# A hybrid decoder layer on one core: fewer warming transposes, the first weights cast in halves, the last operand sum traced later

## The chip, the cores and the metric

The kernel runs on one core of one Trainium2 chip. The metric is the device time of one execution in microseconds, the median of several runs. Engines are named as in the profile: PE is TensorE, DVE is VectorE, ACT is ScalarE, POOL is GpSimd, SP is SyncE, which here issues most transfers.

## The reference

One step of a one-layer decoder over a prompt of 512 tokens and 8 sequences of 4 sampled tokens, with a matrix-memory branch (mLSTM) and a sliding-window attention side by side, gates, a merge and a layer norm. The part that this change touches is the input projection of prompt and samples (544 rows together):

```python
def _in_proj(x, w_in, b_igate, b_fgate):
    u = jnp.einsum('btd,dc->btc', x, w_in)
    ...
    q_m, k_m, v_m, o_m, z_m, q_a, k_a, v_a, z_a, g_m, g_a, i_pre, f_pre = parts
```

`w_in` has 2048 rows and 18952 columns, all in float32.

## The kernel before, in words

**Products.** TensorE is fed with fp32r operands, so each float32 operand is split in a high part, a cast, and a low part, the difference. `split` does this for a weight tile of 8 x 128 rows and 128 columns (`wh` by ACT in L208, `wl` by DVE in L209), and `hilo` for the tokens (L254 and L255). A product is then three matmuls: high by high, high by low, low by high. `wh` and `wl` have two buffers each, so a cast waits until the tile two before it has been used up.

**Tokens first.** The prompt comes in five column pieces (L316): 256, 256, 512, 512 and 512 of its 2048 columns; between them stand the loads of the first weight tiles (`raw`, 512 KB each). PE transposes 128 columns at a time (L337) into one of four PSUM buffers `sm`, and ACT and DVE split them: column blocks 0 to 7 go to `a11` (tokens 0 to 271) and `a21` (the others), blocks 8 to 15 to `xk`. Ahead of all this PE makes warming transposes of a constant (L304), whose result nobody reads.

**Two plain column groups.** The loop at the end of the shown part makes two groups of 128 columns (attention values) by `gemm`: 16 steps over the column blocks, with both halves of the tokens in two PSUM banks. The first group's first weight cast carries `behind`, a pin: the scheduler may not put it before a given cast of the tokens.

**Pairs.** All other columns of `w_in` are made in pairs by `paired`, with seven products in place of eight: the tokens and column blocks are cut in two, and sums of quarters are multiplied (`s1`, `n2`, `n3`, `s4` and the quarters themselves, list `XS`). Step n of a pair uses `XS[n]`; its 24 matmuls of 272 tokens go to one of three banks (`BANK`), several steps add into the same bank, and after each step `gather` evacuates (L704 to L723). Step 4 and step 6 share a bank: step 6 may add only after step 4's evacuation (L719) has read. The sums of tokens are made by the generator `x_sums`: `s1`, `n3`, `n2` while the plain groups run, and `s4` last (L609 to L611), after the mark `plain_done`.

**Order.** What is written in the code is only a preference: a scheduler places the instructions of each engine by priorities (`high_priority`), dependencies and pins (`issue_after`). Generators that were spawned advance one step at each `tick`, so where a generator stands decides the priority of what it issues. On each engine the resulting order is fixed; an instruction that waits holds all behind it.

## Time and profile before

| | |
|---|---|
| median of 3 runs | 2447.45 us (2445.05 to 2449.03) |
| profiled execution | 2445.12 us |
| its span, first to last instruction | 2443.2 us |
| PE busy in the span | 2428.3 us, 99% |
| DVE, ACT, POOL busy | 78%, 51%, 22% |
| TensorE clock granted | 0.999 of full |

The profile belongs to one execution, which is near the lower end of the runs. PE's share is so high that the interest lies in the few places where it waits. In the timeline a row gives the start, the busy time, the engine, the line, the operation, the tiles written and read, the count, and in brackets the idle time before it with what ended it. A busy share of PE does not say that it is at its peak; so the prediction looks at the distance from one matmul to the next.

### The profile page before, as it was taken

To read this page: it belongs to the slowest core of one execution; us is meant where nothing else is said; L and a number is where in the kernel's file an instruction comes from. 1 tells how busy PE (TensorE), PEld (TensorE's weight loads), DVE (VectorE), ACT (ScalarE), POOL (GpSimd) and SP (SyncE) were. 2 spreads that over 40 slices of the span, in tenths; PEclk is the share of its full clock that TensorE was granted. 3 is DMA by queue.
4 is the path that set the end of the run, shared out by engine and by line. 5 is a ranking of instruction groups with operands and counts; after the bars stand their busy time and mean duration, and the time that the engine had idled before them with its cause. 6 is when DMAs were issued, how large, how long until landed. Compare 5 with 4: busy or idle time off the path is not lost.

```text
span 2443.2 us, 49028 instructions
## 1 busy us (share of the span) xinstructions
PE 2428.3 (99%) x19394; PEld 2373.8 (97%) x19394; DVE 1913.3 (78%) x2880; ACT 1251.2 (51%) x2073; POOL 533.4 (22%) x504
## 2 busy tenths in 40 slices
PE   8999999999999999999999999999999999999999
PEld 8999999999999999999999999999999999999998
DVE  7768888888888888887877888878766576877666
ACT  6456676676566665533433444544644444434432
POOL 4114334333333431211111221120000120111111
PEclk9999999999999999999999999999999999999999
DMA  6876666667777655677687676687755598898776
GB/s 180 205 173 157 161 164 145 160 156 174 169 172 177 165 144 146 153 226 235 184 253 235 176 235 216 183 246 222 252 178 191 164 256 241 232 234 270 204 216 204
DMA packets 569501, 479.62 MB, mean 196 GB/s; under 512 B 48632, under 2 KB 464232, under 8 KB 569016
## 3 DMA queue, kind: packets, MB, share of 16 engines
q1 hardware_dynamic: 550520, 410.69, 57.1%
q0 software_dynamic: 17840, 64.23, 13.5%
q8 instruction: 152, 2.49, 0.4%
q10 hardware_dynamic: 912, 1.57, 0.2%
q14 instruction: 77, 0.63, 0.1%
HBM read 326.35 MB, written 100.77 MB: 175 GB/s over the span
## 4 chain that ended last, share of the span: by engine, by line
PE 97%; DMA 1%; DVE 1%; ACT 0%; issue 0%; SPq 0%; DVEq 0%; ACTq 0%
PE bank L694 49%; PE bank L696 24%; PE bank L218 10%; PE sm L1522 2%; PE sm L218 2%; PE bank L1329 1%; PE sm L1556 1%; PE sm L809 1%; PE sm L1572 1%; PE sm L860 1%; PE sm L2011 1%; PE sm L835 1%; PE sm L1334 1%; DMA xr<-in_x_prompt 0%; PE bank L418 0%; DMA kb<-in_state_attn_k 0%
## 5 line engine op out<-in xcount | busy, mean ns | idle before, releaser
L208 ACT CAST wh<-raw 128x1024 fp32r<-128x1024 f32 x641 | 671.8, 1048 | 829.5 <-PE bank L694 718.2
L209 DVE TENSOR_TENSOR wl<-raw,wh 128x1024 fp32r<-128x1024 f32 x641 | 802.0, 1252 | 202.7 <-ACT wh L208 186.6
L694 PE MATMUL bank<-xk,wh 128*128 128x272 f32 x2336 | 323.3, 289 | 0.0
L674 DVE TENSOR_TENSOR raw<-raw,raw 128x1024 f32<-128x1024 f32 x244 | 310.6, 1274 | 7.5 <-DMA raw<-in_w_in 1.9
L694 PEld LDWEIGHTS bank<-xk,wh 128*128 128x128 f32 x2336 | 303.4, 188 | 1.9 <-issue 1.4
L713 POOL TENSOR_TENSOR ev<-p,ev 128x272 f32<-128x272 f32 x85 | 116.8, 1375 | 458.0 <-ACT ev L712 432.8
L696 PE MATMUL bank<-xk,wl 128*128 128x272 f32 x1168 | 170.0, 287 | 0.0
L694 PE MATMUL bank<-n2h,wh 128*128 128x272 f32 x656 | 170.0, 291 | 0.0
L694 PE MATMUL bank<-n3h,wh 128*128 128x272 f32 x656 | 169.5, 291 | 0.2 <-ACT wh L208 0.2
L694 PE MATMUL bank<-s1h,wh 128*128 128x272 f32 x656 | 169.6, 291 | 0.0
L694 PE MATMUL bank<-n2l,wh 128*128 128x272 f32 x656 | 167.9, 287 | 0.0
L694 PE MATMUL bank<-n3l,wh 128*128 128x272 f32 x656 | 167.7, 288 | 0.0
L694 PE MATMUL bank<-s4h,wh 128*128 128x272 f32 x656 | 167.4, 289 | 0.0
L694 PE MATMUL bank<-s1l,wh 128*128 128x272 f32 x656 | 167.3, 287 | 0.0
L694 PE MATMUL bank<-s4l,wh 128*128 128x272 f32 x656 | 167.0, 287 | 0.0
L696 PEld LDWEIGHTS bank<-xk,wl 128*128 128x128 f32 x1168 | 155.6, 188 | 0.1
L672 POOL DMA_DIRECT2D raw<-raw x96 | 83.4, 868 | 314.6 <-DVE ev L721 210.2
L694 PE MATMUL bank<-a11h,wh 128*128 128x272 f32 x584 | 150.4, 289 | 0.0
L694 PE MATMUL bank<-a11l,wh 128*128 128x272 f32 x584 | 149.5, 288 | 0.0
L694 PEld LDWEIGHTS bank<-n3h,wh 128*128 128x128 f32 x656 | 123.4, 188 | 2.1 <-issue 1.2
L694 PEld LDWEIGHTS bank<-s1h,wh 128*128 128x128 f32 x656 | 123.2, 188 | 1.6 <-issue 1.0
L694 PEld LDWEIGHTS bank<-n2h,wh 128*128 128x128 f32 x656 | 123.3, 188 | 1.2 <-issue 1.2
(546 smaller groups left out, 5804.5 us busy)
## 6 DMA issues: line engine op xcount, KB each, us to landing
raw<-in_w_in SPq DMA_DIRECT2D x296, 512.0 KB
raw<-raw POOLq DMA_DIRECT2D x96, 512.0 KB, 5.0
C<-in_state_mlstm_C SPq DMA_DIRECT2D x32, 1024.0 KB
out<-C SPq DMA_DIRECT2D x64, 512.0 KB
raw<-in_w_proj_a SPq DMA_DIRECT2D x32, 512.0 KB
raw<-in_w_proj_m SPq DMA_DIRECT2D x32, 512.0 KB
raw<-in_w_out SPq DMA_DIRECT2D x32, 512.0 KB
d_v<-ev SPq DMA_DIRECT2D x16, 272.0 KB
```

The costliest lines, as they stand in the source:

```text
L208: state["cast"] = A.copy(wh[:, k:k + n], raw[:, k:k + n])
L209: state["split"] = V.tensor_tensor(out=wl[:, k:k + n], in0=raw[:, k:k + n], in1=r32(wh[:, k:k + n]), op=ALU.subtract)
L218: PE.matmul(ps[f][:, :w], a[:, kk], b(k, c, w), start=(k == 0 and n == 0), stop=(k == 15 and n == 2))
L672: G.dma_start(out=w[out][:], in_=w[b][:], accum_op=ALU.add)
L674: V.tensor_tensor(out=w[out][:], in0=w[a][:], in1=w[b][:], op=ALU.add)
L694: PE.matmul(ps, wh[:, k], x(p, k), start=(first and k == 0 and p == 0), stop=False, skip_group_check=True)
L696: state["end"] = PE.matmul(ps, wl[:, k], x(0, k), start=False, stop=(k == 7), skip_group_check=True)
L713: G.tensor_tensor(out=c22, in0=p1, in1=c11, op=ALU.subtract)
L809: PE.matmul(pp[:, c0 + w0:c0 + 256], qs[a][:, j * 128:j * 128 + 128], kx[:, k0:k0 + 256 - w0], start=(n == 0), stop=(n == 1))
L835: PE.transpose(pt[:, b * 128:b * 128 + 128], s_[:, b, 128:256], ident)
L860: PE.matmul(po[:, b * 128:b * 128 + n], VA[:, b], p_[:, 2 * b:2 * b + n // 128], start=(b == 0 and m == 0), stop=(b == 3 and m == 1), skip ...
L1522: state["cells"] = PE.matmul(pp[:, 0:258], a[:, b * 128:b * 128 + 128], b_[:, b, f], start=(b == 0 and n == 0), stop=(b == 3 and n == 2))
```

## The change

Ten warming transposes instead of twenty. The pin of the first weight cast is the cast of column block 2 instead of 3, and that tile is split in two halves of 4 x 128 rows (`parts` 2 for the first half tile of the first group). The last operand sum leaves `x_sums`, becomes a generator of its own, and is spawned with the pairs: its pieces are issued in the ticks of the first pair's steps, each pinned behind the last weight split, and `paired` runs out what is left of it ahead of step 4's product.

```diff
-    for _ in range(20):
+    for _ in range(10):
         PE.transpose(warm[:, 0:128], ident, ident)
...
-                if k == 3:
-                    state["k3"] = state["x_cast"]
+                if k == 2:
+                    state["k2"] = state["x_cast"]
...
-        while not state.get("plain_done"):
-            yield
-        s4 = S["s4"] = quad(act, "s4")
+    def last_sum():
+        s4 = S["s4"]
         for ch in range(4):
...
-            V.tensor_tensor(out=n2r[:, ks_], in0=h12, in1=n2r[:, ks_], op=ALU.subtract)
-            V.tensor_tensor(out=n2r[:, ks_], in0=n2r[:, ks_], in1=l12, op=ALU.add)
+            with tc.issue_after(state["split"].ins):
+                V.tensor_tensor(out=n2r[:, ks_], in0=h12, in1=n2r[:, ks_], op=ALU.subtract)
+                V.tensor_tensor(out=n2r[:, ks_], in0=n2r[:, ks_], in1=l12, op=ALU.add)
             hilo(n2r[:, ks_], s4[0][:, ks_], s4[1][:, ks_])
             yield
...
-                  before=gates_between if kk else None, ps=[sm(), sm()] if kk else None, behind=state["k3"])
+                  before=gates_between if kk else None, ps=[sm(), sm()] if kk else None, behind=state["k2"], parts=(1 if kk else 2, 1))
...
-    state["plain_done"] = True
     for _ in sums_:
         pass
+    S["s4"] = quad(act, "s4")
...
-    paired(work)
+    rest_ = last_sum()
+    spawn(rest_)
+    paired(work, rest=rest_)
```

What this does to the order of the instructions, at the three places that the prediction speaks of. In these rows a number behind a name tells one buffer or use from another; the changed kernel's lines from 603 on are one lower (L718 there is L719 in the profile).

PE at the very beginning, before. `sm_30` to `sm_32` are the transposes of the third column piece, `wh_44` and `wl_45` the first weight tile:

```order
L304 MATMUL sm_13_140<-cc_78 128x128 x20
L337 MATMUL sm_29_223<-cc_78,xr_16_168 128x128 x4
L340 MATMUL bank_25_188<-cc_78,xs_14_161 128x128 x4
L337 MATMUL sm_30_238<-cc_78,xr_18_172 128x128 x4
L218 MATMUL bank_42_369<-a11h_3_114,wh_44_371 128x272
L218 MATMUL bank_43_370<-a21h_5_116,wh_44_371 128x272
L218 MATMUL bank_42_369<-a11l_4_115,wh_44_371 128x272
L218 MATMUL bank_43_370<-a21l_6_117,wh_44_371 128x272
L337 MATMUL sm_31_248<-cc_78,xr_18_172 128x128 x4
```

The same place now (the rows of the first three blocks' transposes, and the repeats of the three products for blocks 1 to 3, are not shown):

```order
L304 MATMUL sm_13_140<-cc_78 128x128 x10
L337 MATMUL sm_29_213<-cc_78,xr_16_158 128x128 x4
L340 MATMUL bank_25_178<-cc_78,xs_14_151 128x128 x4
L218 MATMUL bank_42_359<-a11h_3_114,wh_44_361 128x272
L218 MATMUL bank_42_359<-a11l_4_115,wh_44_361 128x272
L218 MATMUL bank_42_359<-a11h_3_114,wl_45_362 128x272
L218 MATMUL bank_43_360<-a21h_5_116,wh_44_361 128x272
L337 MATMUL sm_30_228<-cc_78,xr_18_162 128x128 x4
```

Before, the third piece's first transposes stood ahead of every product. Now twelve products on `a11` and one on `a21` stand ahead of them. Later in the same queue, from the fifth piece's transposes on, the rows are in the old order.

DVE in the first pair, now, from the split of step 3's weights (`wl_95`) to that of step 6 (`wl_111`). L609 and L610 make the sum `n2r`, L255 with `s4l` its low half, L453 to L461 are small operations of the gates, L714 and L718 are evacuations:

```order
L209 TENSOR_TENSOR wl_95_793<-raw2_84_743,wh_94_792 128x1024
L255 TENSOR_TENSOR s4l_70_715<-n2r_137,s4h_69_714 128x544
L610 TENSOR_TENSOR n2r_137<-n2r_137,xk2_9_120 128x544
L714 SCALAR_TENSOR_TENSOR ev_98_823<-bank_101_836,p1_93_786 128x272
L209 TENSOR_TENSOR wl_100_833<-raw_82_739,wh_99_832 128x1024
L609 TENSOR_TENSOR n2r_137<-xk2_8_119,n2r_137 128x544
L209 TENSOR_TENSOR wl_103_888<-raw2_83_741,wh_102_887 128x1024
L610 TENSOR_TENSOR n2r_137<-n2r_137,xk2_10_121 128x544
L454 RECIPROCAL t_75_720<-t_75_720 128x17
L718 SCALAR_TENSOR_TENSOR ev_98_823<-bank_101_836,ev_98_823 128x272
L209 TENSOR_TENSOR wl_111_939<-raw2_84_743,wh_110_938 128x1024
```

Not shown are further rows of the same kinds: from the split ahead of these (`wl_91`) to L718 there are four splits, eight sums, two low halves and five small operations; the last sum stands between L454 and L718, and the other two low halves behind `wl_111`. Before, no row of the last sum stood here: all twelve were done ahead of the first pair's second split.

PE where the first pair's step 5 (`s4`, `wh_102`) and step 6 (`wh_110`) meet, now:

```order
L693 MATMUL bank_96_797<-s4l_70_715,wh_102_887 128x272
L693 MATMUL bank_96_797<-s4h_69_714,wh_102_887 128x272
L693 MATMUL bank_101_836<-xk2_7_118,wh_110_938 128x272
L693 MATMUL bank_101_836<-xk2_9_120,wh_110_938 128x272
L695 MATMUL bank_101_836<-xk2_8_119,wl_111_939 128x272 x4
L695 MATMUL bank_96_797<-s4h_69_714,wl_103_888 128x272 x8
L693 MATMUL bank_121_1046<-a11h_3_114,wh_114_971 128x272
```

Step 6 was behind all 24 matmuls of step 5. Now nine of step 5 come first, then the 24 of step 6, then the other fifteen of step 5, and behind them the second pair's first product (`wh_114`). On ACT the third and fourth piece's casts (`s4h`) stand behind the cast of `wh_110` and ahead of that of `wh_114`.

## The prediction

> **What bounds the kernel now.** I read the page's first part, the waits of TensorE (PE) over the whole span, and then PE's timeline at the beginning, where all three edits lie.

> ```profile
> PE 2428.3 (99%) x19394; PEld 2373.8 (97%) x19394; DVE 1913.3 (78%) x2880; ACT 1251.2 (51%) x2073; POOL 533.4 (22%) x504
> ```
> ```profile
> PE sm L304 <- DMA cc<-in_consts: 3.4, 1, 3.4
> PE bank L218 <- DVE c L1759: 2.9, 1, 2.9
> PE sm L337 <- DMA xr<-in_x_prompt: 2.3, 1, 2.3
> PE sm L1026 <- DMA kb<-in_state_attn_k: 1.0, 1, 1.0
> PE bank L218 <- DVE xk L255: 0.5, 1, 0.5
> ```

> PE sets the time: all its listed waits together are some 10 us of 2443, and those of the first 200 us are the three on `cc`, `xr` and `xk`. The first ends before any edit can act. So at most 2.3 + 0.5 = 2.8 us can be won here, 0.11%; whatever PE loses in the later steps is lost in full, since it has no other slack.

> ```profile
> 3.37 4.53 PE L304 MATMUL sm<-cc 128*128 128x128 f32 x20 [3.37 <-DMA cc<-in_consts]
> 7.69 2.02 PE L337 MATMUL sm<-cc,xr 128*128 128x128 f32 x16
> 9.54 0.60 PE L340 MATMUL bank<-cc,xs 128*128 128x128 f32 x4
> 12.49 0.63 PE L337 MATMUL sm<-cc,xr 128*128 128x128 f32 x4 [2.34 <-DMA xr<-in_x_prompt]
> ...
> 26.75 0.50 PE L218 MATMUL bank<-xk,wh 128*128 128x272 f32 x2
> 27.75 0.52 PE L218 MATMUL bank<-xk,wh 128*128 128x272 f32 x2 [0.50 <-DVE xk L255]
> ```

> The reader is to see two gates. At 12.49 the third block of prompt columns lands; from there PE is dense until 27.25. At 27.75 it has waited for the low half of column block 12 (`xk`), and from there on it is dense again.

> **Ten transposes fewer.** The twenty start between 3.37 and 7.69, 0.216 us apart. The ten that go are worth 2.2 us on PE, so the first column block's transposes start near 5.5 if their data are there (bounds 5.5 and 7.69; the trace shows only that they did not wait at 7.69). PE then waits longer for what lands at 12.35: alone this edit gives nothing, it lets ACT and DVE begin the column splits earlier.

> **The first weights in halves, behind the third column block.**

> ```profile
> 11.51 1.04 ACT L208 CAST wh<-raw 128x1024 fp32r<-128x1024 f32 x1
> ```
> ```profile
> 12.59 1.23 DVE L209 TENSOR_TENSOR wl<-raw,wh 128x1024 fp32r<-128x1024 f32 x1 [0.61 <-ACT wh L208]
> ```
> ```profile
> 120.00:200.00 80.00, 80.00 (x643) 79.97 (x644) 56.88 (x80) 47.05 (x80) 19.62 (x17) 1.00 0.70 171
> ```

> ACT had no idle time before its cast at 11.51, so the weights had landed by then. With ACT's queue ahead shorter by one column block and begun about 2 us earlier, the cast can start between 9.5 and 11.5; I take 9.7, as these weights are issued between the second block (there by 7.7) and the third (12.4). The halves take about 0.55 us each on ACT (half of 1.04) and 0.62 on DVE, so the first `wh` half is ready near 10.3 and its `wl` half near 10.9. As the rows of the order show, 13 products now stand ahead of the third block's transposes. At 80 us / 643 = 0.124 us each they take 1.6 us, and the last ends near 12.7: the transposes start some 0.3 later than 12.49, but 1.6 us of products are behind PE. That is a lead of 1.3 us (bounds: none if the weights land at 11.4, 2.3 if all of the gap is filled).

> **The lead meets the second gate.** What must come before 27.75 is a chain on other engines:

> ```profile
> 23.74 1.05 ACT L208 CAST wh<-raw 128x1024 fp32r<-128x1024 f32 x1 [1.05 <-DMA raw<-in_w_in]
> ```
> ```profile
> 24.65 1.35 POOL L585 TENSOR_TENSOR n2r<-n2r,r 128x544 f32<-128x544 f32 x1 [0.46 <-DVE r L351]
> ```
> ```profile
> 21.74 0.69 DVE L255 TENSOR_TENSOR xk<-sm,xk 128x512 fp32r<-128x512 f32 x1 [0.37 <-ACT xk L254]
> ...
> 24.88 2.20 DVE L209 TENSOR_TENSOR wl<-raw,wh 128x1024 fp32r<-128x1024 f32 x1
> 27.01 0.68 DVE L255 TENSOR_TENSOR xk<-sm,xk 128x512 fp32r<-128x512 f32 x1
> ```

> DVE's split of the fourth weight tile (`wl_54`) stands ahead of the low half that PE waits for, in the changed order as well. It waits for ACT's cast, and that for a load at 23.7, which hangs on DMA alone. It then took 2.20 us instead of 1.23, because POOL's sum ran from 24.65 to 26.0 beside it. An earlier DVE can lose its 0.37 us gap at 21.74 and let POOL start that much sooner; the cast's end at 24.79 stays. So the low half ends 0 to 0.4 earlier: I take **0.3 us gained**. PE comes to this place 1.3 us sooner and waits there: its wait grows from 0.5 to about 1.5. The further blocks of `xk` are not late:

> ```profile
> 29.75 0.68 DVE L255 TENSOR_TENSOR xk<-sm,xk 128x512 fp32r<-128x512 f32 x1
> ```
> ```profile
> 32.98 0.41 PE L218 MATMUL bank<-xk,wh 128*128 128x272 f32 x2
> ```

> DVE has the last low half by 30.4, and PE comes to its last `xk` rows of this tile at 33.

> **The last sum in the first pair.** Twelve DVE operations of 0.64 us (7.7 us) and four casts leave 40.8 to 51.0 and come between the first pair's splits.

> ```profile
> 41.64 1.99 DVE L609 TENSOR_TENSOR n2r<-xk,n2r 128x544 f32<-128x544 f32 x3
> ...
> 44.18 1.22 DVE L209 TENSOR_TENSOR wl<-raw,wh 128x1024 fp32r<-128x1024 f32 x1
> 45.32 1.98 DVE L610 TENSOR_TENSOR n2r<-n2r,xk 128x544 f32<-128x544 f32 x3
> ...
> 55.41 1.20 DVE L209 TENSOR_TENSOR wl<-raw,wh 128x1024 fp32r<-128x1024 f32 x1
> ...
> 56.53 0.48 DVE L439 TENSOR_SCALAR t<-t,bi 4x544 f32<-4x544 f32 x1
> 57.44 1.23 DVE L209 TENSOR_TENSOR wl<-raw,wh 128x1024 fp32r<-128x1024 f32 x1 [0.42 <-ACT wh L208]
> ...
> 60.37 0.44 DVE L715 SCALAR_TENSOR_TENSOR ev<-bank,p 128x272 f32<-128x272 f32 x1 [0.46 <-PE bank L696]
> ...
> 67.00 0.44 DVE L719 SCALAR_TENSOR_TENSOR ev<-bank,ev 128x272 f32<-128x272 f32 x1 [0.76 <-PE bank L696]
> 67.36 1.22 DVE L209 TENSOR_TENSOR wl<-raw,wh 128x1024 fp32r<-128x1024 f32 x1
> ```
> ```profile
> 66.73 0.29 PE L694 MATMUL bank<-s4h,wh 128*128 128x272 f32 x1
> ...
> 69.73 2.17 PE L694 MATMUL bank<-xk,wh 128*128 128x272 f32 x16
> ...
> 72.74 0.29 PE L694 MATMUL bank<-a11h,wh 128*128 128x272 f32 x1
> ```

> In the cleared stretch DVE wins nothing that PE waits for. Afterwards, from `wl_91` at 55.41 up to the fifth product's evacuation (L719, after: L718), the changed queue holds four splits at 1.14 (44.18 to 45.32), eight sums and two low halves at 0.64, and 1.15 us of small ones: 4.6 + 6.4 + 1.15 = 12.1 us, so L718 runs at 67.5 to 67.95 instead of 67.00. Before, the seventh product, which adds into the same bank, began at 69.73 and had 2.3 us of slack. Now it stands behind nine of the sixth product's 24 matmuls: 66.73 + 9 x 0.124 = 67.85. Undisturbed, PE would wait 0.1 us. The ninth matmul (67.7) needs the sum's third piece: it is finished 0.8 us ahead of L718 in DVE's queue (66.7), and its cast stands on ACT behind `wh_110`:

> ```profile
> 65.93 1.05 ACT L208 CAST wh<-raw 128x1024 fp32r<-128x1024 f32 x1 [1.42 <-PE bank L694]
> ...
> 68.92 1.05 ACT L208 CAST wh<-raw 128x1024 fp32r<-128x1024 f32 x1 [1.95 <-PE bank L694]
> ```

> `wh_110` ends at 67.0, a cast of 544 columns takes 544/1024 of 1.05, so it comes at 67.55, just in time. But POOL's sum of the second product now meets a full DVE:

> ```profile
> 57.84 1.45 POOL L713 TENSOR_TENSOR ev<-p,ev 128x272 f32<-128x272 f32 x1 [2.00 <-ACT ev L712]
> ```

> `wl_95` would start at 58.24, inside it. A split that began 0.23 us after a POOL sum (24.88 behind 24.65) took 2.20 instead of 1.23, 1.0 us more; the split begun before it (57.44) took 1.23. So the bounds are 0.1 and 1.1 us of waiting, and I take **1.1**, as the start inside is the nearer row. [...]

> Last, the next pair's first cast (`wh_114`, 68.92 before) waits for the buffer that the sixth product's weights hold, and their last use is now behind the seventh product. It is covered by the eight `wl_103` matmuls (1.0 us) where 3.8 us lay before (68.92 to 72.74), and takes 1.05 and two hand-overs: 0 to 0.4 us, I take **0.2**. In the second pair DVE catches up.

> **Sum.** -0.3 + 1.1 + 0.2 = +1.0 us, so 2444.2 of span, and 2446.1 beside the profiled execution's 2445.12. That execution is the lower end of the three runs (median 2447.45, 2.3 above it); put on the median, **2448.5 us**.

> **Rivals.**
> - *The lead is kept* (2446.0): the second gate moves as far as PE's lead because the load of 23.7 lands sooner or POOL's sum is out of `wl_54`'s way (up to 1.0 us), and the first pair costs 0.1. That is -1.3 and -0.1 and little back. For it: POOL starts earlier too. Against it: the load. Chance 0.25.
> - *DVE keeps up* (2447.3): the gate swallows the lead and POOL falls beside another operation: -0.3 + 0.1 + 0.1. Chance 0.12.
> - *Slower: the last sum comes due in the open.* Place: DVE between 56 and 71 us. If further splits of the first two pairs meet POOL, PE waits piece by piece; the price is up to all twelve operations, 7.7 us (2455). It decides against "same" once more than 4.9 of the 7.7 are exposed. For it: DVE had only 3.4 of these 15 us free before (5 - 2.94, 5 - 4.54, 5 - 4.10):

> ```profile
> 56.00:61.00 5.00, 5.00 (x42) 5.00 (x41) 2.94 (x6) 2.89 (x7) 2.26 (x2) 1.00 0.59 145
> 61.00:66.00 5.00, 5.00 (x43) 4.99 (x42) 4.54 (x16) 2.40 (x7) 0.00 (x0) 1.00 1.01 216
> 66.00:71.00 5.00, 5.00 (x43) 5.00 (x42) 4.10 (x7) 2.03 (x2) 0.63 (x2) 1.00 0.92 263
> ```

> (The third figure behind the comma is DVE's.) Against it: the small operations of the gates give way, and the sum above exposes 1.1. Chance 0.08, half of it over 4.9.
> - *The edit does not act*: if the weights land near 11.4, the lead is nil, the gate decides all the same, and the time is the forecast's. It shares its chance of 0.55.

> **Numbers.** 0.2% is 4.9 us, about what a measurement of this kernel can tell from no change. The runs before spread from -2.4 to +1.6 about their median. Range: 2443.5 (the kept lead, 2446.0, and a run 2.4 low) to 2452.0 (a first pair worse by 2 us, and a high run). Faster needs more than the 2.8 us that can be won: 0.03, slower 0.04, same 0.93.

> **What would show it.** Right: PE's wait for `xr` at 12.4 gone or short, its wait for `xk` near 27.5 grown to 1 us or more, PE's row that ends it at 27.3 to 27.7, a new PE wait on DVE or ACT near 67 of about 1 us, a small one before the second pair. Wrong: an `xk` row well before 27 (lead kept), no wait near 67, waits of more than 2 us in the first two pairs, or any change behind 200 us that is larger than these.

## The result, and the profile after

The changed kernel took **2455.25 us** (median of 7 runs, 2451.36 to 2457.92) against 2447.45 of before, measured beside it: ratio 1.0032, 95% interval 1.0022 to 1.0042. A second measurement gave 2452.77 (11 runs, 2448.40 to 2455.54) against 2447.27: 1.0018, interval 1.0009 to 1.0027. So by the medians it is slower by 5.5 to 7.8 us, where +1.0 was forecast; the range on record ended at 2452.0. The profiled execution has a span of 2451.2 us (2453.02 us in all), 8.0 longer than that of before.

The first part of the profile's page of the changed kernel, and the waits of its TensorE (PE) over the whole span (us in total, times, longest):

```profile
PE 2432.2 (99%) x19384; PEld 2373.1 (97%) x19384; DVE 1911.1 (78%) x2881; ACT 1252.1 (51%) x2074; POOL 530.9 (22%) x504
```
```profile
PE bank L218 <- DVE ev L722: 2.7, 1, 2.7
PE bank L693 <- ACT wh L208: 1.4, 3, 1.0
PE bank L218 <- ACT wh L208: 1.3, 1, 1.3
PE bank L218 <- DVE c L1760: 1.1, 1, 1.1
PE bank L218 <- DVE wl L209: 1.0, 1, 1.0
PE bank L693 <- ACT s4h L254: 0.7, 1, 0.7
PE bank L218 <- DVE xk L255: 0.7, 1, 0.7
...
PE sm L337 <- DMA xr<-in_x_prompt: 0.5, 1, 0.5
```

The wait of 2.3 for the third column piece of `xr` is gone, as it should be; the 0.5 that is left is another, for the second piece at 7.75. New are also the waits for `ev` (L722), for the casts `wh` in L693 and L218, for `wl` and for `s4h`. Where they stand (PE's timeline of the changed kernel):

```profile
7.75 1.10 PE L337 MATMUL sm<-cc,xr 128*128 128x128 f32 x8 [0.50 <-DMA xr<-in_x_prompt]
...
10.61 0.39 PE L218 MATMUL bank<-a11h,wh 128*128 128x272 f32 x1 [1.32 <-ACT wh L208]
12.15 0.39 PE L218 MATMUL bank<-a11h,wl 128*128 128x272 f32 x1 [1.02 <-DVE wl L209]
...
27.40 0.52 PE L218 MATMUL bank<-xk,wh 128*128 128x272 f32 x2 [0.70 <-DVE xk L255]
...
68.29 0.39 PE L693 MATMUL bank<-s4h,wh 128*128 128x272 f32 x1 [0.74 <-ACT s4h L254]
...
102.38 0.39 PE L693 MATMUL bank<-n2h,wh 128*128 128x272 f32 x1 [1.00 <-ACT wh L208]
...
1751.18 0.79 PE L218 MATMUL bank<-bh,wh 128*128 128x272 f32 x2 [2.73 <-DVE ev L722]
...
1768.81 0.36 PE L218 MATMUL bank<-bh,wh 128*128 128x272 f32 x1 [1.09 <-DVE c L1760]
```

Up to 70 us much of this is the forecast: no wait for the third piece near 12.4, the second gate 0.35 earlier, a wait near 68. Not in it are the waits of 1.32 and 1.02 for the first weight halves, and the wait for `xk` is 0.70 where 1 us or more was expected. The rows at 102 and 1751 are not in it either. Why the halves were late, POOL and DVE of the changed kernel show: the first `wl` half fell beside a POOL sum, and the two took 2.11 us together where 2 x 0.62 were reckoned.

```profile
10.20 1.34 POOL L360 TENSOR_TENSOR n2r<-a11h,a11l 128x544 f32<-128x544 f32 x1 [0.64 <-DVE a11l L255]
```
```profile
10.59 2.11 DVE L209 TENSOR_TENSOR wl<-raw,wh 128x512 fp32r<-128x512 f32 x2
```

**Where the time came from.** Since PE's order is nearly the same in both, each matmul of one trace can be set against the same matmul of the profiled execution of before. The table gives, for one profiled execution of each kernel of this study, the us lost (+) in each stretch of before's time:

| kernel | to 40 | 40-80 | 80-150 | 150-1740 | 1740-1800 | 1800-2425 | to the last matmul |
|---|---|---|---|---|---|---|---|
| changed | -0.3 | 1.0 | 1.9 | -1.1 | 1.1 | 2.4 | 3.3 |
| after_again (the same) | 1.6 | 1.0 | 1.8 | -1.0 | 1.1 | 2.6 | 3.3 |
| after_tail | 0.1 | 0.9 | 1.8 | 0.0 | 1.0 | 0.6 | -0.7 |
| sum_only | 0.3 | 5.6 | 5.0 | -1.1 | 1.2 | 1.0 | 1.7 |
| begin_only | 1.5 | 0.0 | 1.6 | -0.5 | 0.0 | 2.1 | 3.3 |
| begin_fill | -0.5 | 0.0 | 0.1 | 0.6 | -0.3 | 0.2 | 1.7 |
| gates_late7 | 0.9 | 0.0 | 2.2 | -0.9 | -0.1 | 0.1 | 1.7 |
| after_v712 | 3.5 | 0.1 | 6.5 | -0.2 | 1.2 | 1.0 | 1.7 |
| after_pin6 | 3.4 | 3.7 | 0.5 | -0.7 | -1.5 | 0.2 | 1.7 |
| after_v712_pin6 | 2.7 | 3.9 | 1.5 | -1.2 | 0.0 | 0.6 | 1.7 |
| after_gl8 | 1.7 | 0.8 | 1.3 | -1.4 | -0.4 | 1.4 | 1.7 |
| pin6_fill_tail | 0.2 | 6.2 | 0.5 | -1.4 | 0.0 | 0.8 | -0.7 |
| delay24 | 1.7 | 0.0 | 1.1 | -1.4 | -1.6 | 0.0 | 1.7 |
| before_tail | 0.2 | 0.0 | 0.0 | -1.1 | 0.0 | 1.0 | -0.7 |

One execution is one draw, and some of these lie far from their kernel's median (`sum_only` at 2458.67, `after_v712` at 2458.51, `begin_only` at 2452.81), so only what recurs is read as a cause: some 1.0 at 40 to 80, 1.8 to 1.9 at 80 to 150 and 1.1 at 1740 to 1800 in the kernels with the moved sum. The 1.6 of `begin_only` at 80 to 150 is another wait: 1.38 us for `wl` at 99.42, as DVE stood idle for 3.23 us ahead of its weight sum L674; what it waited for the profile does not name. So this stretch can cost as much without the moved sum, and only the row of a wait tells which one it is. The stretch 150 to 1740 holds a wait for a load at 920 us that comes and goes in every kernel, and the end is taken up below.

### The profile page after: what moved, and what is told of

Same layout as the page of the kernel before. It is cut to its first block, busy times and chain, and to the rows that moved or that the text cites. A ratio compares the mean times of both kernels' runs of the same rounds, so it can differ in the third digit from the quotient of the medians.

```text
span 2451.2 us, 49003 instructions
## 1 busy us (share of the span) xinstructions
PE 2432.2 (99%) x19384; PEld 2373.1 (97%) x19384; DVE 1911.1 (78%) x2881; ACT 1252.1 (51%) x2074; POOL 530.9 (22%) x504
## 4 chain that ended last, share of the span: by engine, by line
PE 93%; DMA 2%; DVE 2%; issue 1%; SPq 1%; ACT 1%; POOL 0%; POOLq 0%; DVEq 0%; ACTq 0%
PE bank L693 47%; PE bank L695 23%; PE bank L218 8%; PE sm L1523 2%; PE bank L1328 1%; PE sm L218 1%; PE sm L1557 1%; PE sm L808 1%; PE sm L1573 1%; PE sm L859 1%; DMA raw<-in_w_out 1%; PE sm L2012 1%; DVE wl L209 1%; PE sm L834 1%; PE sm L1333 1%
## 5 line engine op out<-in xcount | busy, mean ns | idle before, releaser
L208 ACT CAST wh<-raw 128x1024 fp32r<-128x1024 f32 (+1 forms) x642 | 671.9, 1047 | 836.9 <-PE bank L693 696.8
L209 DVE TENSOR_TENSOR wl<-raw,wh 128x1024 fp32r<-128x1024 f32 (+1 forms) x642 | 802.0, 1250 | 203.5 <-ACT wh L208 180.5
L693 PE MATMUL bank<-xk,wh 128*128 128x272 f32 x2336 | 323.5, 289 | 0.0
L673 DVE TENSOR_TENSOR raw<-raw,raw 128x1024 f32<-128x1024 f32 x244 | 310.9, 1275 | 14.5 <-PE bank L418 4.6
L693 PEld LDWEIGHTS bank<-xk,wh 128*128 128x128 f32 x2336 | 303.4, 188 | 1.9 <-issue 1.4
L712 POOL TENSOR_TENSOR ev<-p,ev 128x272 f32<-128x272 f32 x85 | 119.7, 1408 | 456.4 <-ACT ev L711 418.8
L693 PE MATMUL bank<-n2h,wh 128*128 128x272 f32 x656 | 170.1, 291 | 1.0 <-ACT wh L208 1.0
L693 PE MATMUL bank<-n3h,wh 128*128 128x272 f32 x656 | 169.4, 291 | 0.2 <-ACT wh L208 0.2
L693 PE MATMUL bank<-s1h,wh 128*128 128x272 f32 x656 | 169.3, 291 | 0.0
L693 PE MATMUL bank<-s4h,wh 128*128 128x272 f32 x656 | 167.7, 289 | 0.9 <-ACT s4h L254 0.7
L693 PE MATMUL bank<-n2l,wh 128*128 128x272 f32 x656 | 168.0, 287 | 0.0
L693 PE MATMUL bank<-s1l,wh 128*128 128x272 f32 x656 | 167.5, 287 | 0.3 <-DVE s1l L255 0.3
L693 PE MATMUL bank<-n3l,wh 128*128 128x272 f32 x656 | 167.6, 288 | 0.0
L693 PE MATMUL bank<-s4l,wh 128*128 128x272 f32 x656 | 167.0, 287 | 0.0
L671 POOL DMA_DIRECT2D raw<-raw x96 | 83.4, 868 | 319.2 <-DVE ev L720 188.3
L693 PE MATMUL bank<-a11h,wh 128*128 128x272 f32 x584 | 150.3, 289 | 0.0
L693 PE MATMUL bank<-a11l,wh 128*128 128x272 f32 x584 | 149.5, 288 | 0.0
L693 PEld LDWEIGHTS bank<-s4h,wh 128*128 128x128 f32 x656 | 123.2, 188 | 2.7 <-issue 1.2
L693 PEld LDWEIGHTS bank<-n2h,wh 128*128 128x128 f32 x656 | 123.4, 188 | 2.4 <-ACT wh L208 1.2
L693 PEld LDWEIGHTS bank<-n3h,wh 128*128 128x128 f32 x656 | 123.4, 188 | 1.9 <-issue 1.2
```

The source lines that it names most:

```text
L208: state["cast"] = A.copy(wh[:, k:k + n], raw[:, k:k + n])
L209: state["split"] = V.tensor_tensor(out=wl[:, k:k + n], in0=raw[:, k:k + n], in1=r32(wh[:, k:k + n]), op=ALU.subtract)
L671: G.dma_start(out=w[out][:], in_=w[b][:], accum_op=ALU.add)
L673: V.tensor_tensor(out=w[out][:], in0=w[a][:], in1=w[b][:], op=ALU.add)
L693: PE.matmul(ps, wh[:, k], x(p, k), start=(first and k == 0 and p == 0), stop=False, skip_group_check=True)
L712: G.tensor_tensor(out=c22, in0=p1, in1=c11, op=ALU.subtract)
```

## The experiments

Times are medians. A ratio is to before, measured beside it, and is estimated from all runs, so it is not exactly the quotient of two medians. `gaps` ran once (2508.70 us) and is read for its clock alone.

| kernel | us (runs) | ratio, 95% interval |
|---|---|---|
| sum_only | 2453.06 (9) | 1.0032, 1.0021 to 1.0044 |
| begin_only | 2447.18 (11) | 1.0005, 0.9996 to 1.0013 |
| delay24 | 2448.68 (11) | 1.0003, 0.9994 to 1.0012 |
| after_tail | 2450.31 (11) | 1.0012, 1.0003 to 1.0021 |
| before_tail | 2445.04 (11) | 0.9994, 0.9986 to 1.0003 |
| gates_late7 | 2449.47 (11) | 1.0011, 1.0003 to 1.0020 |
| after_pin6 | 2450.33 (11) | 1.0015, 1.0006 to 1.0024 |
| before_tail_sm1 | 2446.26 (11) | 0.9999, 0.9991 to 1.0008 |
| after_again | 2452.77 (11) | 1.0018, 1.0009 to 1.0027 |
| after_v712 | 2455.95 (8) | 1.0031, 1.0020 to 1.0041 |
| after_v712_pin6 | 2452.71 (11) | 1.0021, 1.0012 to 1.0030 |
| before_tail_fill | 2447.98 (11) | 1.0004, 0.9995 to 1.0013 |
| begin_fill | 2446.84 (11) | 0.9998, 0.9989 to 1.0007 |
| after_gl8 | 2450.16 (11) | 1.0013, 1.0005 to 1.0022 |
| pin6_fill_tail | 2450.03 (11) | 1.0013, 1.0004 to 1.0022 |

### Which part of the change: sum_only, begin_only

`sum_only` is the changed kernel with the two edits of the beginning undone; `begin_only` has the last sum back in `x_sums`.

```diff
 sum_only
+    for _ in range(20):
...
+                  behind=state["k3"])
 begin_only
+        while not state.get("plain_done"):
+            yield
+        s4 = S["s4"] = quad(act, "s4")
...
+    paired(work)
```

> The kernel before with the last sum moved and nothing else; warming and first weights as before. Theory A (the moved sum alone makes the loss: 2.5 us of PE waits in the first and third pair, and what follows from being late): 2453 to 2456, with the 1.00 us wait for wh of the third pair near 102 us in its trace. Theory B (the beginning has a late cost of its own): 2449 to 2451. Theory C (the loss behind 1700 us is chance of the clock and of the transfers, apart from the edits): the pairs cost 2.5 to 3.5 us, and the rest is there or not whichever edit is in.

> The changed kernel with its last sum put back to where it was: ten transposes and the halves alone. Theory A: 2446.5 to 2447.5, PE 0.3 ahead of before from 28 us to the end. Theory B: 2450 or more with a change of more than 2 us behind 1700 us. Theory C: PE 0.3 ahead up to 200 us, and at the end between 2445 and 2451 as the half clock falls in the last 20 us or not.

The moved sum alone makes the whole slowdown (1.0032), the beginning alone none that can be told (1.0005), though in its profile PE is 1.5 behind at 40 us and not 0.3 ahead. The profile of `sum_only` is one of three of its nine runs that took 2458.7 us or more; the other six took 2450.6 to 2453.1. It shows what the first pair can cost when a transfer comes late (ACT's rows, then PE's):

```profile
69.13 1.04 ACT L208 CAST wh<-raw 128x1024 fp32r<-128x1024 f32 x1 [4.31 <-DMA raw<-raw]
70.08 1.19 ACT L254 CAST s4h<-n2r 128x544 fp32r<-128x544 f32 x2
```
```profile
70.77 0.60 PE L693 MATMUL bank<-s4h,wh 128*128 128x272 f32 x1 [2.58 <-ACT s4h L254]
```

The last pieces of `s4h` stand on ACT behind the cast of step 6's weights, and these come from a transfer that POOL issues. In the changed kernel that issue stands behind a long POOL sum:

```profile
57.51 4.20 POOL L712 TENSOR_TENSOR ev<-p,ev 128x272 f32<-128x272 f32 x1 [2.05 <-ACT ev L711]
61.66 0.87 POOL L671 DMA_DIRECT2D raw<-raw  x1
```

Before, the same sum took 1.45 us. Here the cast at 66.64, 5.0 us behind the issue, just met the landed weights; in `sum_only` the same transfer was issued at 62.31, and the cast came 6.8 us behind it. The other loss there, 5.0 us at 80 to 150, is the gates' (below).

### Is a delay simply added: delay24

```diff
+            if at == 14 and not state.get('put'):
+                state['put'] = 1
+                with tc.issue_after(state['end'].ins):
+                    dt = sm()
+                    for _ in range(11):
+                        PE.transpose(dt[:, 0:128], ident, ident)
```

> The kernel before with eleven transposes of a constant ahead of the third pair's first product, whose result is not read: 11 x 0.216 = 2.4 us of PE and nothing else, about what the pairs cost in the changed kernel. If a delay is simply added: 2449.8. If a program that is 2.4 us late meets later stages worse (Theory A's second half): 2453 to 2456. Theory C: 2449.8 plus 0 to 3.3 by whether the half clock falls in the last 20 us.

The eleven transposes lasted from 96.08 to 97.20, 1.1 us in place of 2.4: they stand 0.10 us apart here, and 0.216 at the start of the program. By the ratio the time rose by 0.7 (interval -1.5 to 2.9): a delay of 1.1 us is added, at most, and not multiplied. The 2.4 us that were meant, about what the pairs cost in the changed kernel, were not tested.

### The end: after_tail, before_tail

```diff
-            PE.matmul(ps[:, 0:c1 - c0], ones1, state["ln_b"][0:1, c], start=True, stop=False)
+            PE.matmul(ps[:, 0:c1 - c0], ident, state["ln_b"][:, c], start=True, stop=False)
```

> The changed kernel with the eight matmuls of one row (1*128, the bias into the last banks) made over 128 rows: the identity times the bias on all partitions, the same sum. If the half clock in the last 15 us (2437.07 to 2443.9 in the changed kernel) comes from these rows being counted as little work, the granted clock stays 1.00 there and the time falls by about 3.3 us to 2452; if it comes from PE's idle stretch at 2439 or from the phase alone, it stays at 2455.

> The kernel before with the eight one-row matmuls near the end made over 128 rows, the same sum; the changed kernel gained 2455.25 - 2450.31 = 4.9 us by it. If the half clock at the end belongs to both kernels alike, this gains as much: 2441 to 2443, and the end is no part of the difference. If it comes mainly in the changed kernel, because its end falls otherwise on the pieces of 3.4 us in which the clock is granted, this gains 0 to 1.5: 2445 to 2447, and 3 to 4 of the 7.8 us lie at the end.

Stretches near the end: span of the stretch, busy us and number of rows of PE, PEld, DVE, ACT and POOL, granted clock of PE, DMA share, GB/s. The changed kernel, and `after_tail`:

```profile
2435.00:2440.00 5.00, 5.00 (x9) 1.76 (x8) 4.90 (x10) 0.40 (x1) 0.98 (x1) 0.71 0.51 169
2440.00:2445.00 5.00, 5.00 (x8) 1.88 (x6) 1.67 (x3) 1.75 (x3) 0.00 (x0) 0.61 0.67 252
```
```profile
2435.00:2440.00 5.00, 5.00 (x13) 2.23 (x12) 4.90 (x10) 1.57 (x3) 0.99 (x1) 1.00 0.43 136
```

With the bias made from one row, the clock is halved in the last products; over 128 rows it is granted in full (0.71 and 0.61 in the two stretches above against 1.00). This holds in 12 of 13 profiles with the one-row matmuls (1.7 or 3.4 us lost) and in none of five without. The one exception is the profiled execution of before on which the sum was built. The half-clock pieces of 3.41 us (last section) fit this: with the one-row matmuls counted as idle, the full-clock piece ahead of the halved one lacks 2.07 us or more of other work in all 12, and in before they fall on two pieces, 1.65 and 1.90 us. So the 3.3 us of the table are that execution's luck with where its pieces lay, and most likely no work of the change. The edit gains 2.5 and 4.9 us on the changed kernel (against its two medians, measured at other times) and 1.5 (interval -0.7 to 3.4) on before; whether the end costs the changed kernel more cannot be told from these.

### The third pair: gates_late7

```diff
-        for _ in range(3):
+        for _ in range(7):
             yield
```

> The kernel before, last sum where it was, but the gates' second half (L471 to L531) four ticks later: L471 stands behind 16 weight splits on DVE, in the changed kernel behind 15, before behind 12. If it is the gates' rows among the third pair's splits and casts that made 1.9 us of PE waits at 97 to 110 us, they come here too: PE 1.5 to 2.5 behind before at 112 us, nothing in the first pair, 2448 to 2450. If the sum's own load does it: no PE wait there and 2446.6.

In before the sum stays, only the gates' second half is late, and the wait of the changed kernel comes back, and one more (PE's timeline of `gates_late7`):

```profile
102.07 0.39 PE L694 MATMUL bank<-n2h,wh 128*128 128x272 f32 x1 [0.86 <-ACT wh L208]
108.53 0.39 PE L694 MATMUL bank<-s4h,wh 128*128 128x272 f32 x1 [0.18 <-ACT wh L208]
144.59 0.39 PE L694 MATMUL bank<-s1h,wh 128*128 128x272 f32 x1 [0.51 <-ACT wh L208]
```

So it is the gates' rows, not the sum's own load, that the third pair pays for. How they stand there, ACT and DVE of the changed kernel:

```profile
98.48 0.66 ACT L513 ACTIVATE t<-t 4x544 f32<-4x544 f32 x1 [1.46 <-DVE t L507]
99.15 0.66 ACT L514 ACTIVATE t<-t 4x544 f32<-4x544 f32 x1
...
101.28 2.00 ACT L208 CAST wh<-raw 128x1024 fp32r<-128x1024 f32 x2 [0.70 <-DVE raw L673]
```
```profile
97.43 0.86 DVE L505 TENSOR_SCALAR t<-t,t 4x128 f32<-4x128 f32 x4
...
99.98 1.21 DVE L673 TENSOR_TENSOR raw<-raw,raw 128x1024 f32<-128x1024 f32 x1
```

ACT's exponentials wait for DVE's L507, DVE's weight sum L673 stands behind the gates' rows, the cast `wh` waits for that sum, PE for the cast. Before, L513 ran at 87.2, in the second pair.

### The banks: after_pin6

```diff
+            with tc.issue_after(state['end'].ins) if at == 6 and not state.get('put') else ExitStack():
                 half_product(w, n)
```

> The changed kernel with step 6 of the first pair pinned behind all of step 5, as the order was before. That also gives back the buffers: 105 of the 309 PSUM banks of the pairs lie elsewhere in the changed kernel, none here. If the banks' places cost the 1.1 us at the stage change, PE's wait for ev (L722, 2.73 us near 1751 us) is gone, the wait for c near 1766 is 2.9 again, and PE's lag does not change there. In the first pair step 5 now waits for the last low halves in the open: 1 to 3 us instead of 1.0. Time 2452 to 2456; if the banks mean nothing, the wait at 1751 stays.

The built program shows why: PSUM banks are handed out as they come free, step 6 ahead of step 5's end changes the order of two of them, and 105 of the 309 uses of `bank` lie elsewhere than before, until the pairs end at 1747 us. There the first plain group then meets the bank of the last evacuation (L722), which stands behind 2.6 us of DVE splits (DVE of the changed kernel):

```profile
1748.06 2.63 DVE L255 TENSOR_TENSOR bl<-pf,bh 128x544 fp32r<-128x544 f32 x4
1750.60 0.43 DVE L722 SCALAR_TENSOR_TENSOR ev<-bank,p 128x272 f32<-128x272 f32 x1
```

With the order back, PE's only wait there is the old one (timeline of `after_pin6`, 1740 to 1772):

```profile
1771.76 0.36 PE L218 MATMUL bank<-bh,wh 128*128 128x272 f32 x1 [2.90 <-DVE c L1762]
```

The wait at 1751 and the 1.1 us are gone. Of the six kernels whose banks moved five show 1.0 to 1.2 there; the sixth, `after_gl8`, has the wait too, but no half clock behind it, which before had at 1766 (0.50 from 1765.76 to 1769.18). The third pair's loss is gone too, as the gates' rows came out earlier; the first pair costs 3.7 instead of 1.0, for step 5 now waits in the open (0.60 and 1.05) and the clock is halved behind it (matmuls 0.226 us apart from 74.77 on, 0.125 before the waits). The time, 2450.33, lies below the 2452 to 2456 that were expected.

### POOL's long sum: after_again, after_v712, after_v712_pin6

`after_again` is the changed kernel itself. `after_v712` makes the first pair's L712 on DVE, and `after_v712_pin6` adds the pin of `after_pin6` to it.

```diff
-            G.tensor_tensor(out=c22, in0=p1, in1=c11, op=ALU.subtract)
+            first, state['first'] = not state.get('first'), 1
+            (V if first else G).tensor_tensor(out=c22, in0=p1, in1=c11, op=ALU.subtract)
```

> The changed kernel once more, beside the two that alter its first pair, so that they are compared on one chip, and for a second profile. If the sixteenth part of POOL's transfer (L671, issued at 61.66 behind the 4.20 us of L712) or the half clock makes its runs spread, this profile has the first pair's cost somewhere between 1.0 and 4.8 us; time 2451 to 2458, median 2453 to 2455.

> The changed kernel with the first pair's L712 on DVE in place of POOL (0.4 to 0.7 us more on DVE, POOL's transfer no longer behind it). If POOL's 4.20 us beside DVE's sums is what makes the first pair dear (its transfer of step 6's weights lands at 66.9 or later, the cast wh_110 and the s4h pieces behind it wait): L671 starts near 58, the cast never waits for it, the first pair costs 0 to 1 us, the median falls by 1.5 to 3. If DVE's load alone is the cause: the first pair costs 1.0 to 2.0 as before and the median stays. The third pair and the stage change (1.1) remain in both.

> Both: L712 on DVE and step 6 behind all of step 5, which gives the banks back and puts the gates' rows behind 13 splits in place of 15. If the three named causes (POOL's transfer, the gates' rows in the third pair, the banks) are the whole, what is left is the first pair's wait for the last pieces of s4 (0.5 to 2 us): 2447 to 2449.5. If something else of the moved sum costs: 2451 or more.

With L712 on DVE the first pair costs 0.1 instead of 1.0 in its profile: this POOL sum is what the first pair paid for, as the prediction's term has it (by which way, see below). But the median did not fall, it is 2455.95. What the first pair won, the second lost (DVE of `after_v712`, then PE):

```profile
84.63 0.64 DVE L462 SCALAR_TENSOR_TENSOR t<-t 128x17 f32<-128x17 f32 x1
...
90.44 1.28 DVE L471 TENSOR_TENSOR_SCAN t<-t,t 4x544 f32<-4x544 f32 x1 [4.98 <-DMA t<-t]
91.65 1.19 DVE L209 TENSOR_TENSOR wl<-raw,wh 128x1024 fp32r<-128x1024 f32 x1
92.77 0.42 DVE L715 SCALAR_TENSOR_TENSOR ev<-bank,p 128x272 f32<-128x272 f32 x1
```
```profile
93.24 0.39 PE L693 MATMUL bank<-n3h,wh 128*128 128x272 f32 x1 [3.28 <-DVE ev L715]
```

L462 finishes the gates' `t`, a transfer turns it, L471 scans it. Before, 5.4 us lay between the two, and the scan did not wait; in the changed kernel it is 2.5:

```profile
65.87 0.18 DVE L462 SCALAR_TENSOR_TENSOR t<-t 128x17 f32<-128x17 f32 x1
...
71.42 1.27 DVE L471 TENSOR_TENSOR_SCAN t<-t,t 4x544 f32<-4x544 f32 x1
```
```profile
81.31 0.17 DVE L462 SCALAR_TENSOR_TENSOR t<-t 128x17 f32<-128x17 f32 x1
...
83.99 1.28 DVE L471 TENSOR_TENSOR_SCAN t<-t,t 4x544 f32<-4x544 f32 x1 [0.49 <-DMA t<-t]
```

That wait was 0.49 and 0.42 in the two profiles of the changed kernel, 3.63 in `sum_only`, 4.98 here: the weight splits queue behind a transfer. What goes with a late transfer is in the same profiles. In three kernels, these two and `after_gl8` below, L462 fell beside POOL's sum of the second pair and took 0.64 to 0.75 us instead of 0.17 or 0.18; both ended together, and the gates' transfer (8.5 KB) was issued 0.11 us behind POOL's 512 KB (POOL and SP of `sum_only`, below). The scan that waits for it began 5.03 and 5.14 us behind its issue. In the six other profiles in which the scan waited, the two transfers were issued 0.74 us or more apart, and the scan began 2.4 to 3.7 us behind. No run takes this apart from other causes.

```profile
87.22 0.85 POOL L671 DMA_DIRECT2D raw<-raw  x1
```
```profile
87.33 0.64 SPq L463 DMA_DIRECT2D t<-t  x1
```

The 2447 to 2449.5 expected of both edits together was missed as well (2452.71): its beginning (2.7) and first pair (3.9) carry half clock.

### The scan out of the transfer's way: after_gl8

The same line as in `gates_late7`, in the changed kernel, with 8 in place of 3.

> The changed kernel with the gates' scan (L471) five ticks later: behind 17 weight splits on DVE in place of 15, so that its transfer has landed when DVE comes to it. If DVE's wait for that transfer makes the spread: L471 has no wait for DMA, no run above 2455, median 2450 to 2452; the gates' rows then meet later pairs and may still cost 1 to 2.5 us there, as in the third. If not: 2453 to 2455 with runs up to 2458.

L471 ran at 89.15 without a wait, 5.3 us behind L462, though its transfer was issued 0.11 us behind POOL's; the median is 2450.16, no run is above 2452.51. The three signs are those of the theory, from one profile and 11 runs. How much of the median the scan's wait makes is not shown: the interval, 1.0005 to 1.0022, overlaps that of the changed kernel's second measurement, 1.0009 to 1.0027.

### Idle PE and the clock: gaps, begin_fill, before_tail_fill, before_tail_sm1

`gaps` adds idle stretches of PE in the pairs, `begin_fill` and `before_tail_fill` put transposes into stretches that were idle, `before_tail_sm1` takes a wait away.

```diff
 gaps, ahead of the first product of pairs 5 to 20 of before
+                for _ in range(1 + at // 7 % 2):
...
+                        PE.transpose(dt[:, 0:128], ident, ident)
+                        A.copy(ident, dt[:, 0:128])
...
+                        state['end'] = PE.transpose(dt[:, 0:128], ident, ident)
 begin_fill, on begin_only, ahead of the first plain group's products
+                    for _ in range(11):
+                        PE.transpose(ps[0][:, 0:128], ident, ident)
 before_tail_fill, on before_tail, ahead of the second late plain group
+                    for _ in range(13):
+                        PE.transpose(dt[:, 0:128], ident, ident)
 before_tail_sm1, on before_tail
-            plain_a(ct, every=(1, 2), prio=0 if ct else AHEAD)
+            plain_a(ct, every=(1, 2), prio=0 if ct else AHEAD, ps=[sm(), sm()] if ct == 1 else None)
```

> The kernel before with 16 idle gaps of PE added, one ahead of each of the pairs 5 to 20: PE transposes, ACT copies the result, PE transposes that copy, once (even pairs, about 1 us idle) or twice (odd pairs, about 2 us or more in two parts). If idle PE brings the half clock: a share of the gaps is followed by a piece of 3.41 us at half clock, more of the long ones than of the short, and none lies between 100 and 500 us away from a gap. If the half clock falls by chance: no such pieces there, as in before (full from 7.90 to 1765).

> Ten warming transposes and the halves, last sum where it was, and eleven transposes of a constant between the column transposes and the first product (11 x 0.216 = 2.4 us), where PE waited 1.32 and 1.02 us for the halves. If idle PE brings the half clock: no half piece between 9 and 19 us, PE's lag at 28 us between -0.4 and +0.5, and the median 0.5 to 1.5 below begin_only's 2447.18. If it comes from the fewer warming transposes alone: half pieces stay, 2447.2.

> The kernel before with the 128-row matmuls at the end, and thirteen transposes of a constant (13 x 0.216 = 2.8 us) into the 2.90 us wait at the stage change near 1765 us. If idle PE is what brings the half clock, the piece of 3.41 us at 1765 to 1769 is granted in full and the time falls by 1.7 from 2445.0 to 2443.3; the wait itself stays as long as it was. If the clock falls there for another reason, it stays at 2445.

> The last-rows kernel on the base of before, and besides the second plain group of the late projection (the one that waits 2.90 us for c near 1765 us) in two banks of the other pool, so that it need not wait. If the wait is the bank's alone: 2.9 us less than the kernel with the 128 rows alone, and 1.7 more where the half clock came behind it (1765.76 to 1769.18 before). If the attention, which shares that pool, then waits, it comes back there and the two are equal.

A gap of `gaps`, in stretches of some 3.41 us, two of them cut where the clock changed (188.24 and 191.65; columns as above):

```profile
181.40:184.83 3.43, 3.43 (x29) 3.43 (x28) 3.43 (x5) 2.36 (x6) 1.62 (x2) 1.00 0.54 174
184.83:188.24 3.41, 1.23 (x11) 0.99 (x10) 2.13 (x4) 3.40 (x5) 0.00 (x0) 1.00 0.99 219
188.24:191.65 3.41, 3.41 (x17) 3.41 (x17) 0.71 (x1) 0.17 (x1) 0.00 (x0) 0.50 0.71 203
191.65:195.07 3.42, 3.42 (x30) 3.42 (x30) 1.96 (x3) 1.95 (x3) 1.07 (x1) 1.00 0.17 51
```

PE is idle for 2.18 us of one piece of 3.41, and the next piece has half the clock: 17 rows of matmuls where 30 fit. The first gap of each kind came out under 1 us. Of the other seven single gaps of 2.18 us six lead to this; the seventh lies across two pieces. Of the other seven double ones, 1.71 and 1.09 us and so mostly divided over two pieces, one does. The lengths came out otherwise than expected (the single gap holds the longer stretch), but for these gaps the question is answered: idle PE brings it, and what counts is the idle time within one piece. In its profile `begin_fill` has no half piece at its beginning and is 0.5 ahead of before at 40 us; `before_tail_fill` cut the idle stretch at the stage change to 1.39 us and its half piece is gone. Neither gains in time that can be told, nor does `before_tail_sm1`. At the stage change `before_tail_fill` won back 1.5 of 3.3 us that it had lost at 922, and then lost 5.4, by a wait of 3.54 for a load at 1990 and the half piece behind it. `before_tail_sm1` was rid of the 2.90 wait and of the half piece, and gave the gain back in four waits of 0.45 to 1.80 between 1863 and 1982; the second theory of the last expectation (it comes back elsewhere) is nearer. The changed beginning of `after_again`, in the same pieces:

```profile
9.14:12.55 3.41, 1.29 (x10) 0.83 (x8) 3.08 (x6) 3.25 (x11) 2.10 (x2) 1.00 1.04 384
12.55:15.97 3.42, 3.42 (x15) 3.42 (x16) 1.35 (x4) 1.13 (x5) 2.23 (x2) 0.50 1.12 345
15.97:19.38 3.41, 3.41 (x31) 3.41 (x30) 2.66 (x7) 3.07 (x11) 1.81 (x3) 1.00 1.12 318
```

Its two new waits, 1.10 for `wh` and 1.02 for `wl`, fall into one piece. Six of the eight profiles with the changed, unfilled beginning are slowed between 9 and 19 us, one of eight with the old one; in the mean they are 1.8 and 0.5 behind at 40 us. In two of the six (`after_pin6`, `after_v712`) the clock did not fall but rose only at 19.05 and 19.04 us (17 matmuls between 14 and 17.5 us in each, 31 in the kernel before); there PE waited 0.54 and 0.61 us for `xr` right behind the ten transposes, and twenty, at 0.216 us each, would have lasted to 7.7. So the two waits are one cause and the fewer transposes may be another; `begin_fill` undoes both and does not part them. In times all this is within the error (`begin_only` 1.0005, `begin_fill` 0.9998).

### All named causes undone: pin6_fill_tail

The edits of `after_pin6`, `begin_fill` and `after_tail` in one kernel.

> The changed kernel with the beginning filled, step 6 behind step 5 (banks back, gates' rows two splits earlier) and the last rows over 128 rows. If the named causes are the whole: first pair 2 to 3.7 us (with its half piece), nothing at 100 to 110, nothing at the stage change, no half piece at the beginning or in the last products: 2446.5 to 2449. If something else of the change costs: 2450 or more.

Beginning 0.2, third pair 0.5, stage change 0, end -0.7, as expected; but the first pair cost 6.2 (waits of 2.1 and 1.0 us, and 3.4 us for two half pieces), and the time is 2450.03, above the range given and at the border of the other theory. In this one profile what is left of the slowdown stands in the first pair, which the pin that brings the banks back makes dearer; that no further cause is at work is likely by it, and not shown.

No version is faster than before beyond its interval; the nearest is `before_tail`, 0.9994 (0.9986 to 1.0003).

## Why the prediction was wrong

- **Beginning.** The -0.3 is right in the first profile: the second gate at 27.40, 0.3 ahead behind it. The way there is not. The halves came at 10.6 and 12.15 where 10.3 and 10.9 were reckoned, the second because POOL's sum of 10.20 stood beside it (2.11 us for the two splits): the collision that the prediction priced in the first pair came here, where it had none. So the third piece's transposes, behind the 13 products, began at 13.63 and not near 12.8, the lead was 0.5 us in place of 1.3, and the wait for `xk` 0.70 in place of 1.5. In six of the eight profiles with this beginning the new waits or the fewer transposes slow the clock as well: some +1.3 in the mean of the profiles where -0.3 stood, which the times neither show nor exclude.
- **First pair.** The place and the size were right: 1.0, 1.0, 0.9 and 0.8 us in four profiles for a term of 1.1 + 0.2, and 0.1 without POOL's L712. The mechanism was not, so that the sizes agree is luck. DVE's split beside POOL's sum was not lengthened (1.21 us at 57.88; 1.0 more was reckoned), L718 was not late (67.22; 67.5 was reckoned undisturbed), and PE had no wait ahead of the second pair (73.40). It is POOL's sum that was longer, 4.20 us instead of 1.45, and the transfer queued behind it came later (issued at 61.66, before at 59.25); its landing then decides when ACT casts step 6's weights, and `s4h` behind them (0.74 us of PE; in `sum_only` the pair cost 5.6, of which two half pieces make 3.4). The prediction had the sign of it in hand: POOL's 1.45 us at 57.84 were for 272 columns, the 1.35 at 24.65 for 544, so the sum that began under a running split (57.44) was much the longer for its size.
- **"In the second pair DVE catches up."** This is the step that failed. The gates' small rows do give way, as the prediction says itself, and they do not vanish: 12 us later the scan has lost its distance to a transfer and the rest stands among the third pair's sums and casts, where nothing was reckoned. It cost 1.8 to 1.9 us in three profiles with the same order, and more when the transfer is late: 5.0 in `sum_only`, and 6.5 in `after_v712`, with a half piece in it.
- **Nothing behind 200 us.** Wrong for a reason that is in no row of the order: the banks, a wait of 2.73 us at 1751 and 1.1 us in all. A change of this size behind 200 us is what the prediction itself named as a sign of being wrong.
- **Waits priced by their own length.** Two us or more of idle PE within one piece of 3.41 us cost 1.7 more each time (22 of 22 pieces, last section); none of the prediction's prices had it.
- **The base.** The profiled execution was set on the median by adding 2.3. It is the one profile with the one-row matmuls and no half piece among the last products, worth 1.7 or 3.3 us in the others, so this step held.

Named so far: 1.3 + 1.0 + 1.8 + 1.1 = 5.2, against 5.5 and 7.8 measured. This is a sum of stretches of single profiles, the first of them a mean, and so an estimate. The rest may be the executions in which a transfer is late; how often that is, the profiles (one of each kernel) do not say. Whether the end and the waits for loads near 920, 2120 and 2405 us differ between the kernels stays open.

The rival "the last sum comes due in the open" named the right size (up to 2455) and the right place to begin with, with a chance of 0.08; its reason against, that the gates' rows give way, was the mechanism that failed.

## What to carry to other kernels

Work moved into a stage that has room on average pushes out whatever had the lowest priority there: follow those rows to where they land, and look at what they then stand in front of, above all if one of them waits for a transfer. When the order of two uses changes, buffers taken from a ring or a free list can move for the rest of a stage; the built program's addresses tell it before any run. And with one core and PE at 99%, price a wait not by its length alone but by whether, with its neighbours, it fills a good half of a clock piece (here 2.0 us of 3.41).

## What the runs showed of the hardware

The POOL sum L712 took 4.19 or 4.20 us in all seven profiles where DVE's sums stood beside it in the first pair, and 1.45 before, while DVE's split beside it, at 57.88, took 1.21. It began at 57.51 inside a DVE sum and ended at 61.71, just behind a DVE evacuation (61.10 to 61.54). DVE's rows in the changed kernel:

```profile
57.24 0.71 DVE L610 TENSOR_TENSOR n2r<-n2r,xk 128x544 f32<-128x544 f32 x1
57.88 1.21 DVE L209 TENSOR_TENSOR wl<-raw,wh 128x1024 fp32r<-128x1024 f32 x1
...
60.37 0.71 DVE L610 TENSOR_TENSOR n2r<-n2r,xk 128x544 f32<-128x544 f32 x1
```

POOL ended 0.63 us behind the last of these sums in all seven profiles, and before it ended 0.62 behind the one split beside it (57.44 to 58.67). So its own work is about 0.6 us, an estimate, and the rest of the 4.20, some 3.6 us, lies beside a row of DVE operations that follow one another without a gap; that POOL waits for this row to end is read from these ends, and no run shows the wait itself. Where POOL came first, DVE's split was the longer one: 2.20 us instead of 1.23 behind the sum of 24.65 in the kernel before, and 2.11 us for two halves behind that of 10.20 in the changed one, where 0.62 each was reckoned. The prediction let POOL come first because it looked only at the split behind it.
